# A decoder layer on one core: the gated sum's second half is turned by VectorE and DMAs instead of TensorE, and what follows goes token tile by token tile

## The chip, the core and the metric

The kernel runs on one core of a Trainium2 chip. Weights and activations start in HBM; TensorE multiplies into PSUM, VectorE and ScalarE work on SBUF and PSUM, GpSimd does a little of the attention's preparation, and SP issues nearly all DMAs. The metric is the device time of one execution in microseconds, the median of several runs.

## The reference

One layer on x with 256 tokens and 1024 channels, in float32:

```
h = RMSNorm(x)
x_rnn, g_rnn, q, k, v, g_A, g_B = split(h @ W_in)         # 1024 columns each
A = GeLU(g_rnn) * RG-LRU(causal_conv4(x_rnn))
B = causal attention, 8 heads of 128, q and k normalised  # 256 tokens: one block
y = sigmoid(g_A) * (A @ P_A) + sigmoid(g_B) * (B @ P_B)   # the gated sum
x = x + y @ W_out
h = RMSNorm(x)
x = x + (GeLU(causal_conv3(h @ W_up)) * (h @ W_gate)) @ W_down   # 2816 wide
```

## The kernel before

**Products.** Float32 precision comes from three products. Each number is split into a high part hi (rounded to the short format fp32r that TensorE multiplies) and the rest lo, and a product is hi·hi + hi·lo + lo·hi (`mm3`). A weight chunk is 128x2048 numbers (1 MB): SP loads it as `raw`, ScalarE casts it to `hi`, VectorE subtracts to get `lo`. There are three buffers for raw, four for hi, three for lo. Activations are split in the same way; their parts have names that end in h and l (xgh and xgl, mh and ml, h2h and h2l).

**The start.** `g`, the weights of the first norm (4 KB), is loaded by ScalarE's queue; xT, the transposed input, and the first chunks of the k weights come in small pieces (`raws`) by SP's queue. The first activation, `xgh`, is xT times g, rounded; `xgl` is the rest. While these arrive, TensorE runs 9 warm-up products (`warm`). An explicit load of ScalarE's table for the exponential is one of the first operations recorded.

**Units.** `UNITS` (line 33) lists TensorE's work up to the output projection, one unit per chunk. rx, rg and ri belong to the recurrent branch; q, k, v and the heads' attention to the other; ga and gb are the gates, pr and pa the two branches' projections, wo the output projection. pr, pa and wo have four units each: two halves of the output columns, times two halves of the contraction. A unit has four quarters of 12 products of 128x512. `AFTER` (line 35) says which other pieces of work follow which quarter.

**The gated sum.** pr's columns are gated into `sga`, pa's into `sgb`, and `pa_evac` adds them, both token tiles (t = 0, 1; 128 tokens each) of one half of the columns at a time. wo needs the sum channel by channel on the partitions, so it is turned. The first half goes by `m_turn`: VectorE transposes 32x32 blocks (`md`), four DMAs write them to HBM (`mm`), one reads them back in order. The second half goes by `m_t`, TensorE: 2 times 4 transposes of 128x128 into PSUM (`mT`), each set followed by a cast (mh) and a subtraction (ml) from there. These transposes stand among the products of wo0.

**Behind it.** wo0 and wo1 give the first 512 output columns, wo2 and wo3 the others; VectorE adds them to `xs`. The second norm's input is turned too, the first half of token tile 0 by blocks and DMAs (`hd`, `hm`), that of tile 1 by four TensorE transposes (`h2T`, item n10), from which VectorE makes `h2q`, ScalarE `h2h` and VectorE `h2l`. They are needed by up00, the first unit of the feed-forward part, whose units are up (W_up), gt and the seven-product scheme qA, qB, qC (W_gate), and dn or acc (W_down).

**What sets the order.** Nothing is issued as the code is read. Class `Later` records every operation, TensorE's in one list and all others in another, and `issue` (line 238, in the changed kernel 257) walks through `ORDER`: "+n" stands for the next n TensorE operations, every other number is a recorded operation. So all instructions have the line of `issue`, each engine runs its own in the order of this table, and the pools choose buffers by it. Loads that ScalarE's tables need, where none was asked for, are put in ahead of an activation by the compiler.

Of the kernel before, what the change touches and what calls it, by code (L numbers as in the profile page):

```python
# [14 lines left out]
P = 128  # L15
# [18 lines left out]
         "gb1 gb2 gb3 pr0 pr1 pr2 pa0 pa1 pr3 pa2 pa3 wo0 wo1 wo2 wo3")  # L34
# [60 lines left out]
    "pa2.3": "ms",  # L95
    "pa3.2": "s38",
# [10 lines left out]
    "wo0.1": "m2",  # L107
    "wo0.2": "m3",
    "wo1.0": "s40",
    "wo2.0": "s41",  # L110
    "wo2.1": "n10",
# [3 lines left out]
0 4 1 3 26 28 30 32 2 29 31 +2 5 33-34 +1 7 37-38 6 35-36 +2 8 39-40 +1 10 43-44 9 41-42 +3 47-48 11 45-46 12 49-50 13  # L115
51-52 +5 15 55-56 +5 14 53-54 +13 16 59-60 57-58 18 63 17 65-66 64 61-62 19 67-68 +5 23 74-77 +3 20 224-226 69 24 27
227 25 228-235 71 105-106 236-242 +58 93 72 108 21-22 78 109 79-91 +1 96 +5 99 +37 73 142-143 92 102 95 97 94 117-118
120 119 121-122 243 123-126 244 127-133 +9 110 +3 111-112 101 103-104 187-188 107 190 +9 141 +5 116 115 113-114 98 100
144-156 +10 186 +3 191 157-159 245-247 160 248-254 70 255-262 +20 168 +1 170 169 171-172 175 174 173 135 134 136
204-205 +24 207-208 +10 176-177 182-183 199 184-185 195-197 178-180 200 198 201-202 181 162 161 163 +11 212 +3 213 189  # L120
210-211 137 203 192 139 138 206 +16 222-223 +22 220-221 193-194 267 263 271 264 268 140 166 275-276 +7 282 284 +3 285
269 272 265 270 283 277-278 273-274 219 266 +18 302 +6 304 303 294 299 209 297 295 165 167 164 327 298 279 316 300 +25
281 296 286 280 317-318 +20 301 442 305-306 309 +3 307 334-335 310 330-331 308 214 366 454 367-368 370 369 371-378 315
288 311 314 312-313 215 329 379-382 +6 443 332 339 +6 364 319 321 +6 323 362 324 +6 340 +6 217 338 218 328 +19 342 325
343 444 320 326 322 448 333 452-453 455 216 341 +20 336 357 +3 598 337 358 363 599 612 615 +12 356 +15 360-361 445 +9
359 +12 348-349 346-347 351 461 350 352-353 462 365 344-345 463-468 291 289 355 290 354 398-399 613 469-470 446 434
287 397 410 +26 614 435 +8 437 +2 433 +11 383-384 471-475 +3 393 386 394 385 +3 395-396 387 438 556 617 +11 400-401
389 388 402-403 390-392 494 496-497 495 404 498 292 436 +11 411 447 440 412-416 449 616 421-422 417-420 +11 423
405-406 426 522-524 503 526 525 476-477 424-425 427 +26 441 459 428-430 432 431 407-408 439 +1 456 +2 506 509 508 533
507 510 460 450-451 500 458 409 536-537 539 538 521 +1 293 457 +17 478-480 489 481-482 499 504-505 +4 825 824 540 +18  # L130
490 484 483 485 487 486 551-552 555 488 544 554 553 +13 511-515 534 492 517 502 501 649 535 531-532 516 +3 663 527 +3
529 518 493 +15 491 +8 545 528 542 520 519 530 546-547 648 583 585 587 584 586 548 557 +23 558 543 +9 564 +3 565 +5
569-573 559 549-550 650 567-568 +11 566 600 541 +11 588 575 651 589-590 574 579 576 578 577 580 601 560 602 604 562
# [108 lines left out]
def trunk_layer(ctx: ExitStack, tc: tile.TileContext, xT, x, vec, win_fm, win_tm, wri, wpr, wpa,  # L242
# [1099 lines left out]
```

## Time and profile before

| | |
|---|---|
| time, median of 3 runs | 420.74 us (420.3 to 420.89) |
| profiled execution, first to last instruction | 418.6 us |
| TensorE busy | 414.0 us, 1892 matmuls |
| VectorE busy | 360.9 us, 449 instructions |
| ScalarE busy | 307.5 us, 399 instructions |
| GpSimd busy | 61.0 us |
| DMA traffic | 106.89 MB, mean 255 GB/s |
| table loads on ScalarE | 14, 1283 ns each |

The profile has no end-to-end time of its own for the profiled execution beside its span of 418.6 us; the runs' median is 2.14 us above that. In the rows, "x48" is the number of instructions in a group or in a row of equal ones, and "[2.16 <-DMA xT<-in_xT]" says how long the engine was idle before and what ended it. A row of the chain of waits has its start and its length in us. PE is TensorE, DVE VectorE, ACT ScalarE, POOL GpSimd; SPq and ACTq are the queues that issue DMAs.

### The profile page before, as it was taken

How to read it: one execution, taken by the hardware profiler on the slowest of the kernel's cores; microseconds unless marked ns; L12 is line 12 of the kernel's file. 1: busy time of each engine (PE TensorE's matmuls, PEld its weight loads, DVE VectorE, ACT ScalarE, POOL GpSimd, SP SyncE). 2: the span in 40 equal slices, each digit the busy share in tenths (PEclk: the TensorE clock that was granted, in tenths of full speed). 3: DMA queues.
4: the chain of work that ended last, by engine and by line, in shares of the span. 5: the costliest groups of instructions: out<-in, count | busy, mean ns of one | idle time of the engine just before them, and what ended most of it. 6: DMA issues, size and time to landing. Idle time of an engine off the chain costs nothing.

```text
span 418.6 us, 5425 instructions
## 1 busy us (share of the span) xinstructions
PE 414.0 (99%) x1892; PEld 344.4 (82%) x1892; DVE 360.9 (86%) x449; ACT 307.5 (73%) x399; POOL 61.0 (15%) x109
## 2 busy tenths in 40 slices
PE   8999999999999999999999999999999999999996
PEld 7888888888888888888888888888888888888885
DVE  4877699999999999879896789899999989988863
ACT  4787478799989998796144475699897779866630
POOL 0084780009382002000000000000000000000000
PEclk9999999999999999999999999999999999999999
DMA  7998688979696988797698669575799748649803
GB/s 230 416 397 280 194 258 266 321 241 365 220 317 236 279 277 289 221 357 256 205 353 281 233 200 315 173 219 171 258 328 317 279 152 267 205 148 267 318 2 102
DMA packets 46108, 106.89 MB, mean 255 GB/s; under 512 B 8448, under 2 KB 22656, under 8 KB 43648
## 3 DMA queue, kind: packets, MB, share of 16 engines
q1 hardware_dynamic: 45360, 106.01, 76.1%
q10 hardware_dynamic: 720, 0.53, 0.4%
q8 instruction: 15, 0.25, 0.2%
q14 instruction: 13, 0.11, 0.1%
HBM read 92.63 MB, written 13.89 MB: 254 GB/s over the span
## 4 chain that ended last, share of the span: by engine, by line
PE 98%; DMA 1%; ACT 0%; DVE 0%; SPq 0%; issue 0%; ACTq 0%
PE acc L238 14%; PE up L238 13%; PE k L238 5%; PE gb L238 5%; PE qA L238 5%; PE pr L238 5%; PE wo L238 5%; PE ga L238 5%; PE v L238 5%; PE q L238 5%; PE pa L238 5%; PE rg L238 5%; PE rx L238 5%; PE qC L238 3%; PE gt L238 3%; PE last L238 3%
## 5 line engine op out<-in xcount | busy, mean ns | idle before, releaser
L238 DVE TENSOR_TENSOR lo<-raw,hi 128x2048 fp32r<-128x2048 f32 (+1 forms) x64 | 141.4, 2215 | 9.2 <-ACT hi L238 8.3
L238 ACT CAST hi<-raw 128x2048 fp32r<-128x2048 f32 (+1 forms) x64 | 118.2, 1856 | 29.2 <-DMA raw<-in_wout 16.7
L238 PE MATMUL up<-hi,h2l 128*128 128x512 f32 x80 | 31.1, 389 | 0.0
L238 PE MATMUL up<-hi,h2h 128*128 128x512 f32 x80 | 31.1, 389 | 0.0
L238 PE MATMUL up<-lo,h2h 128*128 128x512 f32 x80 | 31.1, 389 | 0.0
L238 PE MATMUL acc<-hi,fah 128*128 128x512 f32 x78 | 30.4, 390 | 0.0
L238 PE MATMUL acc<-hi,fal 128*128 128x512 f32 x78 | 30.4, 389 | 0.0
L238 PE MATMUL acc<-lo,fah 128*128 128x512 f32 x78 | 30.4, 389 | 0.0
L238 POOL TENSOR_TENSOR rsq<-rsq 128x8 f32<-128x8 f32 x32 | 21.0, 655 | 46.7 <-DVE rsq L238 44.5
L238 ACT ACT_TABLE_LOAD x14 | 18.0, 1283 | 1.4 <-PEq L1332 1.2
L238 PEld LDWEIGHTS up<-hi,h2h 128*128 128x128 f32 x80 | 15.0, 188 | 3.2
L238 PEld LDWEIGHTS up<-hi,h2l 128*128 128x128 f32 x80 | 15.0, 188 | 3.1
L238 PEld LDWEIGHTS up<-lo,h2h 128*128 128x128 f32 x80 | 15.0, 188 | 3.1
L238 PEld LDWEIGHTS acc<-hi,fah 128*128 128x128 f32 x78 | 14.6, 188 | 3.1
L238 PEld LDWEIGHTS acc<-lo,fah 128*128 128x128 f32 x78 | 14.6, 188 | 3.1
L238 PEld LDWEIGHTS acc<-hi,fal 128*128 128x128 f32 x78 | 14.7, 188 | 3.1
L238 DVE TENSOR_TENSOR loq<-wq,hiq 128x1024 fp32r<-128x1024 f32 x12 | 14.5, 1215 | 1.3 <-ACT hiq L238 1.3
L238 ACT ACTIVATE fu<-fupd,pv 128x256 f32<-128x256 f32 x32 | 15.2, 502 | 0.5 <-DVE fc L238 0.3
L238 ACT CAST hiq<-wq 128x1024 fp32r<-128x1024 f32 x12 | 12.3, 1049 | 4.1 <-PE acc L238 2.2
L238 DVE TENSOR_TENSOR wq<-wq,wq 128x1024 f32<-128x1024 f32 x12 | 14.6, 1216 | 0.2
L238 DVE TENSOR_TENSOR lot<-wq,hit 128x1024 fp32r<-128x1024 f32 x12 | 14.4, 1218 | 0.0
L238 ACT CAST hit<-wq 128x1024 fp32r<-128x1024 f32 x12 | 12.2, 1045 | 1.0 <-PE acc L238 1.0
(303 smaller groups left out, 1175.3 us busy)
## 6 DMA issues: line engine op xcount, KB each, us to landing
raw<-in_win_fm SPq DMA_DIRECT2D x16, 1024.0 KB, 7.0
raw<-in_wdown SPq DMA_DIRECT2D x11, 1024.0 KB, 6.1
raw<-in_wup SPq DMA_DIRECT2D x10, 1024.0 KB, 5.9
raw<-in_win_tm SPq DMA_DIRECT2D x8, 1024.0 KB, 6.7
wq<-in_wgate SPq DMA_DIRECT2D x16, 512.0 KB, 6.2
raw<-in_wpr SPq DMA_DIRECT2D x4, 1024.0 KB, 7.6
raw<-in_wpa SPq DMA_DIRECT2D x4, 1024.0 KB, 7.8
raw<-in_wout SPq DMA_DIRECT2D x8, 512.0 KB, 5.4
```

What stands on the lines that cost most here:

```text
L238: getattr(engine, name)(*map(real, a), **{n: real(v) for n, v in k.items()})
```

## The change

It has five parts.

1. `m_t` is gone. For each token tile t there is `m_tile_turn(t)`, which is one VectorE transpose of 128x512 in blocks of 32x32, four DMAs to HBM and one back (by `turn_tile`, which the second norm uses already), and `m_tile_split(t)`, a cast and a subtraction of 128x512 from SBUF. TensorE loses eight transposes.
2. pa's second half and the output projection go token tile by token tile: pa2.0 pa3.0 pa2.1 pa3.1, then wo0 (both tiles) wo2.0 wo1.0 wo2.1 wo1.1 wo3.0 wo3.1; a unit with ".t" has 12 products. Tile 0's turn follows pa3.0, tile 1's pa3.1. `pa_evac` and `norm2` take single tiles.
3. up00 does token tile 1 first.
4. h2T is moved from wo2.1 to wo3.0, that is from 36 products ahead of up00 to 18.
5. `ORDER` is written anew from end to end, so all engines' orders change in many places.

The table moves one operation of ScalarE's start. Operation 4, the explicit table load, stood second ("0 4 1 3"); now it stands behind operations 687 and 690 ("687 690 +2 4 +1 689"). In the rows that follow, a number behind a name tells tiles apart, and DMAHW0, DMAHW1 and so on are the counters of eight DMA lanes, which transfers take in turn. ScalarE's first rows before:

```order
L238 DMA g_77<-in_vec 128x8
L238 ACT_TABLE_LOAD
L238 ACTIVATE xgh_95<-xT_93,g_77 128x256 [waits DMAHW2_49,DMAHW0_49]
L238 CAST his_89<-raws_82 128x512 [waits DMAHW3_49]
L238 CAST his_89<-raws_82 128x512 [waits DMAHW4_49]
```

and now:

```order
L257 DMA g_79<-in_vec 128x8
L257 ACT_TABLE_LOAD [waits DMAHW1_49]
L257 ACTIVATE xgh_96<-xT_85,g_79 128x256 [waits DMAHW0_49]
L257 CAST his_91<-raws_87 128x512 [waits DMAHW3_49]
L257 ACTIVATE xgh_96<-xT_85,g_79 128x256 [waits DMAHW4_49]
```

The load that now stands ahead of xgh is one that the compiler put there, and it carries a wait for lane 1, which is g's transfer; xgh is left with the wait for lane 0, xT's. SP now issues xT ahead of the first raws.

VectorE's rows from the end of the first pa half to the product of pa3 (lo_2081 in the change and lo_2059 before are pa3's chunk, the lo_2076 of the change is wo0's; wt, loq and wq belong to W_gate's product), before:

```order
L238 STREAM_TRANSPOSE md<-sgb_1640 128x8x4x32 [waits DVE_49]
L238 TENSOR_TENSOR wt_2054<-wq_2012,wq_1467 128x1024 [waits DMAHW5_49]
L238 TENSOR_TENSOR loq_2056<-wq_1961,hiq_1963 128x1024
L238 TENSOR_TENSOR wq_1961<-wq_1465,wq_1959 128x1024 [waits DVE_49]
L238 TENSOR_TENSOR lo_2059<-raw_2008,hi_2010 128x2048 [waits DMAHW4_49,Activation_49]
L238 TENSOR_TENSOR sga_1398<-pr_1924,sga_1398 128x512 [waits PE_49]
L238 TENSOR_TENSOR sga_1398<-pr_1928,sga_1398 128x512 [waits PE_49]
L238 TENSOR_TENSOR lo_2115<-raw_2016,hi_2113 128x2048 [waits DMAHW7_49,DMAHW0_49,Activation_49]
L238 TENSOR_TENSOR lo_2120<-raw_2014,hi_2118 128x2048 [waits DMAHW5_49,DMAHW6_49,PE_49,Activation_49]
```

and now:

```order
L257 STREAM_TRANSPOSE md<-sgb_1616 128x8x4x32 [waits DVE_49]
L257 TENSOR_TENSOR lo_2076<-raw_1994,hi_2044 128x2048 [waits DMAHW5_49,DMAHW4_49,Activation_49]
L257 TENSOR_TENSOR lo_2081<-raw_2021,hi_2073 128x2048 [waits DMAHW7_49,PE_49,Activation_49]
L257 TENSOR_TENSOR sga_1455<-pr_1906,sga_1455 128x512 [waits PE_49]
L257 TENSOR_TENSOR sgb_1852<-pa_2064,sgb_1852 128x512 [waits PE_49]
L257 TENSOR_TENSOR sga_1455<-pr_1902,sga_1455 128x512
L257 TENSOR_TENSOR sgb_1852<-sgb_1852,sga_1455 128x512 [waits DVE_49]
L257 STREAM_TRANSPOSE md_2134<-sgb_1852 128x4x4x32 [waits DVE_49]
```

pa3's lo stood behind three operations of W_gate's product and stands now behind wo0's lo; the eviction, addition and turn of the second half's tile 0 follow it.

VectorE's rows between wo's evictions and up00 (h2q, h2l: the turned input of the second norm; lo_2297 in the change and lo_2280 before are up00's chunk), before:

```order
L238 TENSOR_TENSOR h2q<-h2T_2273,pv 128x4x128 [waits PE_49]
L238 TENSOR_TENSOR lo_2280<-raw_2209,hi_2254 128x2048 [waits DMAHW3_49,Activation_49]
L238 TENSOR_TENSOR h2l_2299<-h2q,h2h_2297 128x4x128 [waits PE_49,Activation_49]
L238 SCALAR_TENSOR_TENSOR h2l_2299<-hd_2228,pv,h2h_2297 128x128 [waits DMAHW4_49,Activation_49]
L238 SCALAR_TENSOR_TENSOR h2l_2299<-hd_2228,pv,h2h_2297 128x128 [waits Activation_49]
L238 SCALAR_TENSOR_TENSOR h2l_2299<-hd_2228,pv,h2h_2297 128x128
L238 TENSOR_TENSOR xs<-wo_2259,xs 128x512 [waits PE_49]
```

and now:

```order
L257 TENSOR_TENSOR xs<-wo_2161,xs 128x512 [waits PE_49]
L257 TENSOR_TENSOR lo_2297<-raw_2252,hi_2261 128x2048 [waits DMAHW7_49,Activation_49]
L257 TENSOR_TENSOR xs<-wo_2197,xs 128x512 [waits PE_49]
L257 TENSOR_TENSOR h2q<-h2T_2290,pv 128x4x128
L257 TENSOR_TENSOR h2l_2315<-h2q,h2h_2311 128x4x128 [waits Activation_49]
L257 TENSOR_TENSOR xs<-wo_2240,xs 128x512 [waits PE_49]
L257 STREAM_TRANSPOSE hd<-xs 128x4x4x32 [waits DVE_49]
```

h2q now stands behind a lo and behind the eviction of wo3.0 (xs<-wo_2197); before, it stood ahead of both.

The diff, without the greater part of `ORDER`:

```diff
-         "gb1 gb2 gb3 pr0 pr1 pr2 pa0 pa1 pr3 pa2 pa3 wo0 wo1 wo2 wo3")
+         "gb1 gb2 gb3 pr0 pr1 pr2 pa0 pa1 pr3 pa2.0 pa3.0 pa2.1 pa3.1 wo0 wo2.0 wo1.0 wo2.1 wo1.1 wo3.0 wo3.1")
...
-    "pa2.3": "ms",
-    "pa3.2": "s38",
+    "pa20.3": "ms",
+    "pa30.3": "mt0",
+    "pa31.2": "s38",
+    "pa31.3": "mt1",
...
-    "wo0.1": "m2",
-    "wo0.2": "m3",
-    "wo1.0": "s40",
-    "wo2.0": "s41",
-    "wo2.1": "n10",
+    "wo0.3": "s40",
+    "wo20.3": "ms0",
+    "wo10.0": "s41",
+    "wo21.3": "ms1",
+    "wo30.1": "n10",
...
-0 4 1 3 26 28 30 32 2 29 31 +2 5 33-34 +1 7 37-38 6 35-36 +2 8 39-40 +1 10 43-44 9 41-42 +3 47-48 11 45-46 12 49-50 13
...
++1 0 +3 2-3 5-6 30 +3 29 33 7 20 31 +1 32 9 35 +2 37 +1 47 8 41 12 +1 10 +2 11 224 +1 39 +4 43 14 34 +1 36 225 38 +1 49
...
++1 837 +7 656 +3 669 682 +3 683 +6 684 +4 707 777 685 +3 686 +11 25 +4 680 +1 708 +1 678 681 679 +3 687 690 +2 4 +1
...
-    def pa_evac(g, ps):
-        for t in range(2):
+    def pa_evac(g, ps, ts=range(2)):
+        for t in ts:
             m = tok(sgb, g, t)
             nc.vector.tensor_mul(m, ps[t], m)
             nc.vector.tensor_add(m, m, tok(sga, g, t))
...
-    def m_stat(a, k, t):
-        return head_q(a, k, t) if k < 4 else a[k][:, t * P:(t + 1) * P]
-
-    def m_t(c):
-
-        ps = fm_ps(f"mT{c}")
-        for k2 in range(2):
-            cs = slice((2 * (c % 2) + k2) * P, (2 * (c % 2) + k2 + 1) * P)
-            for t in range(2):
-                nc.tensor.transpose(ps[:, k2, t * P:(t + 1) * P], tok(sgb, c // 2, t)[:, cs], ident)
-        split2(mh.pair(c), ml.pair(c), ps)
+    turned_m1, mid_m1 = half("md1"), dram.tile([P, 1024], F32, tag="turn", name="mm1")
+
+    def m_tile_turn(t):
+        turn_tile("mm1", turned_m1, tok(sgb, 1, t), mid_m1, t)
+
+    def m_tile_split(t):
+        v = lambda a: a.half(1).rearrange("p (u i b) -> p u i b", u=8, i=4)[:, 4 * t:4 * t + 4]
+        split2(v(mh), v(ml), by_tile(turned_m1)[:, 4 * t:4 * t + 4])
...
-    def norm2(hf, ps):
-        for t in range(2):
-            nc.vector.tensor_add(xs[:, t, halves[hf]], ps[t], xs[:, t, halves[hf]])
+    def norm2(t, ps):
+        nc.vector.tensor_add(xs[:, t, halves[1]], ps, xs[:, t, halves[1]])
...
+        if (kind, p, kh) == ("up", 0, 0):
+            for q in range(4):
+                for k4 in (2 * (q % 2), 2 * (q % 2) + 1):
+                    tm_mm(open_ps[kind, p], c, k4, k4, h2h, h2l, True, ts=(1 - q // 2,))
+                yield
+            return
```

More of the change, by code (lines that the diff above doesn't have):

```diff
@@ L153 @@
[L153 to L156 removed]
+1 0 +3 2-3 5-6 30 +3 29 33 7 20 31 +1 32 9 35 +2 37 +1 47 8 41 12 +1 10 +2 11 224 +1 39 +4 43 14 34 +1 36 225 38 +1 49
@@ L157 @@
+805 884 843 +7 820-821 +1 887 +2 852 860 888 +2 859 +1 822 +4 912 +2 890 1045 +1 873 +1 826 +5 853 +2 855 +2 914 +1
[5 rows of a table added]
+982 +2 951 +3 949 +2 958 +8 1017 +3 1005 +1 952 +2 954-955 +2 985 +3 960 +2 1062 1050 908 933 +1 1056-1057 +2 961 +2
+984 +3 1075 1051 1048-1049 +4 1014 +7 1073 1063 +2 965 +2 1064 1058 983 +1 1041 +1 986 +2 964 +4 1065 +3 1074 +1 1066
[10 rows of a table added]
 """
@@ L303, in trunk_layer @@
               "pr": lambda c: two(wpr, 0, c), "pa": lambda c: two(wpa, 0, c), "wo": lambda c: by_columns(wout, c)}
-    units = [(u[:-1], int(u[-1])) for u in UNITS.split()]
-    chunk = {u: add(source[u[0]](u[1])) for u in units}
+    units = [(u[:2].rstrip("0123"), int(u.split(".")[0][-1]), *map(int, u.split(".")[1:])) for u in UNITS.split()]
+    chunk = {}
+    for u in units:
+        if u[:2] not in chunk:
+            chunk[u[:2]] = add(source[u[0]](u[1]))
     NP = NF // 2
@@ L882, in run_unit @@
             g, kh = c // 2, c % 2
-            if not kh:
+            if not kh and ts in ((), (0,)):
                 open_ps[kind, g] = [bank(f"{kind}{g}{t}") if kind in ("pa", "rx") else
@@ L887, in run_unit @@
             args = (*{"pr": (yah, yal), "pa": (ybh, ybl), "wo": (mh, ml)}.get(kind, (xgh, xgl)),
-                    kind not in ("q", "v", "wo"), *((m_stat,) if kind == "wo" else ()))
-            if (kind, c) == ("wo", 1):
-                for q in range(4):
-                    for k4 in (2 * (q % 2), 2 * (q % 2) + 1):
-                        tm_mm(ps, i, 4 * kh + k4, k4, *args, ts=(q // 2,))
-                    if q % 2:
-                        norm2_tile(q // 2, ps[q // 2])
-                    yield
-                return
-            for k4 in range(4):
-                tm_mm(ps, i, 4 * kh + k4, k4, *args)
-                if kh and k4 == 3:
+                    kind not in ("q", "v", "wo"), *((head_q,) if kind == "wo" else ()))
+            for k4 in range(4):
+                tm_mm(ps, i, 4 * kh + k4, k4, *args, **({"ts": ts} if ts else {}))
+                if kh and k4 == 3 and ts:
+                    if kind == "pa":
+                        pa_evac(g, ps, ts)
+                    elif g:
+                        norm2(ts[0], ps[ts[0]])
+                    else:
+                        norm2_tile(ts[0], ps[ts[0]])
+                elif kh and k4 == 3:
                     evac[kind](g, ps) if kind in evac else qk_evac(kind, g, ps)
@@ L919, in trunk_layer @@
             item[f"{n}{h}"] = lambda fn=fn, h=h: fn(h)
-    for n in (2, 3):
-        item[f"m{n}"] = lambda n=n: m_t(n)
+    for t in range(2):
+        item[f"mt{t}"] = lambda t=t: m_tile_turn(t)
+        item[f"ms{t}"] = lambda t=t: m_tile_split(t)
     item["mt"], item["ms"] = m_turn, m_split
@@ L1005, in trunk_layer @@
     item["ht"], item["hs"] = h2_turn, h2_split
-    for kind, c in units:
+    for kind, c, *ts in units:
         if (kind, c) not in (("k", 1), ("k", 2), ("k", 3)):
-            run(f"{kind}{c}", run_unit(kind, c))
+            run("".join(map(str, (kind, c, *ts))), run_unit(kind, c, *ts))
     def norm2_stats():
```

65 lines of the change are left out of this document (22 added, 43 removed), and 34 rows, old and new, of the table ORDER.

## The prediction

> **What bounds the kernel now.** I read the page's busy times first, then the list of TensorE's waits, then the chain of waits; their rows stand below in this order.
>
> ```profile
> PE 414.0 (99%) x1892; PEld 344.4 (82%) x1892; DVE 360.9 (86%) x449; ACT 307.5 (73%) x399; POOL 61.0 (15%) x109
> ...
> PE warm L238 <- DVE ones L238: 1.0, 1, 1.0
> PE k L238 <- ACT xgh L238: 0.4, 1, 0.4
> ...
> 5.16 22.51 PE k L238 x96
> ...
> 217.30 2.73 PE wo L238 x12
> 220.03 0.44 PE mT L238 x4
> 220.46 1.40 PE wo L238 x6
> 221.86 0.44 PE mT L238 x4
> 222.30 9.56 PE wo L238 x42
> 231.86 0.44 PE h2T L238 x4
> 232.29 8.21 PE wo L238 x36
> 240.51 16.32 PE up L238 x72
> ```
>
> TensorE is busy 414.0 of 418.6 us. It waits twice, both times before 5.16 us; from then on one product follows the other. So the time is the moment of the first k product, plus the work of TensorE, plus a short tail. Whatever leaves TensorE's queue is won whole; whatever starts k later is lost whole; anything else counts only where it makes TensorE wait.
>
> **What the change takes from TensorE.** It drops the eight mT transposes, which stand between wo products. From 217.30 to 231.86 pass 14.56 us, with 12 + 6 + 42 = 60 wo products in them. One product takes 10.88/48 = 0.2267 us where nothing disturbs it:
>
> ```profile
> 206.42 10.88 PE pa L238 x48
> ```
>
> 60 of them are 13.60 us, so the transposes and the changes to and fro cost 14.56 - 13.60 = **0.96 us**. No other TensorE work is added or removed: token tile by token tile, pa2, pa3 and wo1 to wo3 have the same products in another order, and the four h2T transposes are only moved. The gain is 0.96 us and, since TensorE never waits now, cannot be more in this place.
>
> **What the change does to the start.** The rewritten table moves one ScalarE operation that has nothing to do with attention: the explicit load of the exponential's table stood second, ahead of everything, and now stands far back, in the pa products. Some table must be there for the first activation, xgh, so a load is put just ahead of it, and that load takes over one of xgh's two waits: the one for g (the norm's weights). The timeline of the start before, and the row of g from the list of transfers (size, us from issue to landing):
>
> ```profile
> 0.71 0.41 ACTq L238 DMA_DIRECT2D g<-in_vec  x1
> 1.03 3.68 PE L238 MATMUL warm<-ones 128*128 128x128 f32 x18 [1.03 <-DVE ones L238]
> 1.15 1.28 ACT L238 ACT_TABLE_LOAD   x1 [1.15 <-PEq L1332]
> 4.60 0.51 ACT L238 ACTIVATE xgh<-xT,g 128x256 fp32r<-128x256 f32 x1 [2.16 <-DMA xT<-in_xT]
> 4.66 0.69 DVE L238 TENSOR_TENSOR los<-raws,his 128x512 fp32r<-128x512 f32 x1
> 5.16 0.73 PE L238 MATMUL k<-his,xgh 128*128 128x512 f32 x2 [0.45 <-ACT xgh L238]
> 5.27 0.48 DVE L238 SCALAR_TENSOR_TENSOR xgl<-xT,g,xgh 128x256 fp32r<-128x256 f32 x1
> 6.90 0.73 PE L238 MATMUL k<-his,xgh 128*128 128x512 f32 x2
> ...
> g<-in_vec ACTq DMA_DIRECT2D x1, 4.0 KB, 3.6
> ```
>
> Before, the 1.28 us of the load lay under the transfers, and xgh waited 2.16 us longer. Now the load waits itself. g is issued at 0.71 and lands 3.6 later, at 4.31; it cannot land later than 4.60, when xgh read it. So the load runs from 4.31 to 5.59. How soon an activation follows a load is shown by two later rows of ScalarE's timeline:
>
> ```profile
> 121.86 1.28 ACT L238 ACT_TABLE_LOAD   x1
> 123.16 1.06 ACT L238 ACTIVATE gr<-gr 128x1024 f32<-128x1024 f32 x1
> ```
>
> 0.02 us. Then xgh takes 0.51, to 6.12, and the first product starts 0.05 later (5.11 to 5.16 before), at **6.17 us: 1.01 later**. VectorE follows: xgl began 0.16 after xgh's end, so 6.28 to 6.76; los, which before was finished ahead of xgl, is now queued behind it and ends at 7.45. Products five and six need los: the fifth starts at 7.50, the seventh at 7.95 instead of 6.90, 1.05 later. TensorE waited for nothing behind that in k, and everything ahead of the later products has a microsecond more now, so the rest keeps its pace.
>
> I take **+1.00 us**. Bounds: +1.3 if g lands only at 4.60; below, nothing at all, if g were there by 3.3 us and the load ended as xT lands. The row for g says 4.31, so the value lies near the upper end.
>
> The Trainium skill, "ScalarE: Activation LUTs", section "What ACT_TABLE_LOAD costs", puts a switch at about 1.28 us of load and 1.38 us of drain. The load agrees with the 1.28 here; a drain ahead of the next activation doesn't show in the 0.02 us above. By the page the start would come another 1.38 later, and the sum would be 422.2.
>
> **What the change adds on the other engines.** Two VectorE transposes of 128x512 come (0.71 each, by the row of hd<-xs below); the two casts and two subtractions of this half of m keep their number and size. SP gets ten DMAs, eight writes and two reads like those of hm and hd below. The windows of before, by stage:
>
> ```profile
> core 0: us, PE busy (x) PEld busy (x) DVE busy (x) ACT busy (x) POOL busy (x), PEclk, DMA share, GB/s
> 200.00:232.00 32.00, 32.00 (x148) 26.49 (x147) 27.62 (x27) 12.31 (x10) 0.00 (x0) 1.00 0.81 268
> 232.00:262.00 30.00, 30.00 (x135) 24.84 (x134) 25.07 (x37) 18.47 (x29) 0.00 (x0) 1.00 0.76 264
> ...
> 303.00:345.00 42.00, 42.00 (x186) 34.71 (x186) 39.68 (x33) 33.82 (x40) 0.00 (x0) 1.00 0.79 273
> ```
>
> VectorE is idle for 9.3 of the 62 us from 200 to 262, so 1.42 us more fit. What covers them is slack between a result and its product, and the change uses that up at four places. I give times as without the later start, which moves all of it alike. Durations come from the groups of instructions, the timelines and the list of transfers:
>
> ```profile
> L238 DVE TENSOR_TENSOR lo<-raw,hi 128x2048 fp32r<-128x2048 f32 x10 | 22.8, 2286 | 0.2 <-ACT hi L238 0.2
> L238 DVE STREAM_TRANSPOSE hd<-xs 128x512 f32<-128x512 f32 x3 | 2.1, 711 | 0.1
> ...
> 200.34 1.37 DVE L238 TENSOR_TENSOR sgb<-pa,sgb 128x512 f32<-128x512 f32 x2 [2.31 <-PE pa L238]
> ...
> 202.94 1.25 DVE L238 STREAM_TRANSPOSE md<-sgb 128x1024 f32<-128x1024 f32 x1
> ...
> 227.92 1.78 SPq L238 DMA_DIRECT2D hm<-hd  x4
> ...
> hm<-hd SPq DMA_DIRECT2D x4, 64.0 KB, 1.8
> hd<-hm SPq DMA_DIRECT2D x1, 256.0 KB, 3.1
> ...
> 233.11 0.68 DVE L238 TENSOR_TENSOR h2q<-h2T,pv 128x512 f32<-128x512 f32 x1
> 233.83 0.62 ACT L238 CAST h2h<-h2q 128x512 fp32r<-128x512 f32 x1 [2.59 <-DVE h2q L238]
> 235.91 0.69 DVE L238 TENSOR_TENSOR h2l<-h2q,h2h 128x512 fp32r<-128x512 f32 x1
> ```
>
> First, pa3's first token tile comes 12 products (2.72 us) earlier, at 206.42 + 2.72 = 209.14, and its lo is needed 0.23 later. VectorE does the first half's eviction and addition from 200.34 to 202.94, its turn to 204.19, then two lo of 2.29 that overlap a little, the second of them this one: done near 208.7. Slack 0.6.
>
> Second, the turn of tile 0: pa's second half for it ends at 211.86; eviction, an sga product, addition and transpose are four operations of about 0.7; the four writes take 1.78 to issue and the last of them 1.8 to land, the read 3.1, the cast 0.62, the subtraction 0.69: about 222.5, needed at 225.9. Slack 3.
>
> Third, tile 1: it starts at 217.30, its way back waits in SP's queue behind a wup chunk, and its subtraction stands on VectorE behind the eviction of wo1's first tile (wo1.0 ends at 228.18): done about 230.3, needed at 231.35. Slack 1.
>
> Fourth, h2T is moved from 36 products ahead of up00 to 18. up00 would start at 240.51 - 0.96 = 239.55. Its h2q stands on VectorE behind a lo (2.29, from about 234.4 to 236.7) and behind the eviction of wo3.0, which ends 12 products earlier, at 236.83: eviction to 237.6, h2q 0.68, h2h on ScalarE 0.62, h2l 0.69: h2h near 238.9, h2l near 239.6, needed at 239.55 and 240.0. Slack 0.4 to 0.7, where before h2l was done at 236.6 for a product at about 241, over 4 us ahead.
>
> I cost all four at nothing. Cover gone, each is a stall of its own length; behind 303 us VectorE is busy 39.68 of 42, so a lo that is late once stays late, but its number of operations there is unchanged.
>
> **Sum.** 418.6 - 0.96 + 1.00 = 418.64 us of span. The median, 420.74, lies 2.14 above the profiled span; with it, **420.8 us**: no change.
>
> **The rivals.** (A) *The start costs nothing*: g is there early enough, and the load ends when xT lands. Then 420.74 - 0.96 = 419.8, faster. For it: SP's first transfers come in another order, and with less traffic beside it g may land sooner; against it: the 3.6 us of its row, on its own queue, and nothing that moved on that queue. 17 of 100.
>
> (B) *up00 waits for h2l*, slower. Place: the fourth one above. If the lo ahead of h2q begins one operation late (its hi is cast from a chunk whose load is queued behind the turn's way back on SP), the chain moves by up to a lo, 2.29, less the slack of 0.5: up to 1.8 us, and the same mechanism can hit at the first or third place with 1.7 and 1.3. It decides from 0.8 us of stall on. Time 421.6 to 423, middle 422.2. For it: slack under 1 us at three places where nothing was tight before; against: every chain still closes on paper. 27 of 100.
>
> (C) *The clock falls back.* Between the end of the warm products (4.71) and the first k product TensorE idles 1.45 us instead of 0.45. If the clock falls to half for 3.4 us, 7.5 products take 0.45 instead of 0.227: +1.7, 422.5. Every row of before shows PEclk 1.00, and no gap like it. 5 of 100. The Trainium skill, "TensorE: Matmul & The Clock Gate", section "What's actually happening", speaks of about 3.4 us of idling before the clock drops, by which this gap is too short; no run so far shows either.
>
> (D) *A pause behind the load*: xgh waits once more as long as the load took, 1.28 us, at the start, where nothing covers it: 420.8 + 1.3 = 422.1. The 0.02 us at 123.16 speaks against it. 4 of 100. It is the drain of the Trainium skill's page "ScalarE: Activation LUTs", section "What ACT_TABLE_LOAD costs".
>
> **How the numbers follow.** The forecast, TensorE's gain given back at the start and no stall above 0.5, has 47 of 100: 420.8, its own range 420.2 to 421.5. A has 17, B 27, C and D 9. A change of 0.2%, 0.84 us, is about what a measurement here can tell from none: faster means under 419.90, slower over 421.58. A gives faster, 0.17; the forecast gives no change, 0.47, and B, C and D slower, 0.36. The range leaves out the upper part of B and the lower of A: 419.7 to 422.6.
>
> **What would show it.** In the changed profile: no mT rows; the first table load waits for g's transfer and starts near 4.3 instead of 1.15, xgh near 5.6, the first k product near 6.2; from there to up00 about 0.96 less than the 235.35 of before (5.16 to 240.51). TensorE's waits then list k behind xgh with about 1.4 us. If up, pa or wo stands in that list with 0.8 us or more, B is right; if k starts by 5.3, A; if the granted clock of the first 10 us is under 1.00, C; if xgh begins over 1 us behind the load's end, D.

## The result: about one per cent slower

The changed kernel takes 424.74 us (424.72 to 425.01), the kernel before 420.78 us beside it: a ratio of 1.0097, 95% interval 1.0083 to 1.0112. The forecast was 420.8, its range 419.7 to 422.6: too low, and the range doesn't hold the time.

The profiled execution has a span of 422.9 us, 4.3 more than before. Its page, the busy times:

```profile
PE 415.2 (98%) x1884; PEld 343.0 (81%) x1884; DVE 359.4 (85%) x451; ACT 305.2 (72%) x397; POOL 55.8 (13%) x109
```

The eight transposes are gone (1884 products, 1892 before), but the busy time didn't fall by 0.96 us, and the idle time of TensorE grew from 4.6 to 7.7 us. (A product that waits for its weights can count as busy, so the two numbers belong together.) The list of waits of the changed kernel (what waited, for whom, us in total, times, the longest), TensorE's products first, then its weight loads:

```profile
PE k L257 <- ACT his L257: 1.5, 1, 1.5
PE s L257 <- ACT sm L257: 1.1, 2, 0.7
...
PE k L257 <- DVE his L257: 0.6, 1, 0.6
...
PEld k L257 <- ACT his L257: 3.3, 5, 1.9
PEld s L257 <- ACT sm L257: 1.6, 2, 1.0
...
PEld acc L257 <- DVE lo L257: 0.6, 2, 0.4
```

k, the scores `s` and, a little, `acc` (W_down's products) wait; up, pa and wo don't. The chain of waits of the changed kernel (start, length, what), a part of k and then the place of the change:

```profile
4.02 6.70 DMA raws<-in_win_tm
10.73 8.67 DMA raws<-in_win_tm
...
21.78 8.90 PE k L257 x38
...
211.16 10.88 PE pa L257 x48
222.04 17.68 PE wo L257 x78
...
240.16 4.10 PE wo L257 x18
244.26 16.32 PE up L257 x72
```

Before, k's 96 products stood in this chain as one row from 5.16 on; now loads of k's weights stand in it up to 19.40. The time is best followed by the first product of each group, read from the timelines of the two kernels (us):

| first product of | before | after | difference | since the row above |
|---|---|---|---|---|
| k | 5.16 | 5.32 | +0.16 | +0.16 |
| rx | 27.51 | 30.52 | +3.01 | **+2.85** |
| pr (behind the gates and most of attention) | 171.75 | 176.49 | +4.74 | **+1.73** |
| wo | 217.14 | 221.88 | +4.74 | 0 |
| up | 240.34 | 244.10 | +3.76 | **-0.98** |
| acc (W_down) | 314.14 | 317.93 | +3.79 | +0.03 |
| last (the final chunk) | 352.39 | 356.49 | +4.10 | **+0.31** |
| end (the final products) | 413.86 | 417.93 | +4.07 | -0.03 |

Behind that another 0.24 us come (4.31 of span). They aren't the table's: in every profile of the changed computation here, whichever order it has, the span ends 5.00 to 5.02 us behind the start of the first `end` product, in every profile of the computation before 4.76 to 4.78 us. So the change wins what it takes from TensorE, and the rewritten table loses five times that at places that have nothing to do with the change's first four parts: 2.85 us within k, 1.73 at the gates, 0.31 at W_down.

These rows compare one execution with one. The 93 timed executions of the kernel before have spans from 418.5 to 419.6 us, the middle at 419.0; the profiled one, with 418.6, is among the shortest. So a difference against it, here and below, can lie some 0.3 us too high, and the medians, 3.96 us apart, are the better measure of the whole.

**The start.** The changed kernel's timeline (start, length, engine, operation, idle time before it and what ended it):

```profile
3.19 1.28 ACT L257 ACT_TABLE_LOAD   x1 [3.19 <-DMA xT<-in_xT]
4.48 0.51 ACT L257 ACTIVATE xgh<-xT,g 128x256 fp32r<-128x256 f32 x1
4.75 0.43 DVE L257 CAST his<-raws 128x512 fp32r<-128x512 f32 x1 [3.75 <-DMA raws<-in_win_tm]
...
5.32 0.70 PE L257 MATMUL k<-his,xgh 128*128 128x512 f32 x2 [0.57 <-DVE his L257]
```

The load of the table waits for xT, not for g. The prediction and the section on the change took lane 1 for g's; the lanes are counted in the order of issue, so g has lane 0 and xT, now SP's first transfer, lane 1. xT lands at 3.1, and the load begins at 3.19; before, as SP's second transfer, xT ended xgh's wait at 4.60. So the load lies behind xT, and yet xgh begins 0.12 us earlier than before. A wait for g would have cost nothing either. Its row in the changed kernel:

```profile
g<-in_vec ACTq DMA_DIRECT2D x1, 4.0 KB, 2.6
```

Issued at 0.73, g is there at 3.33, a microsecond earlier than before (3.6 from its issue). The load had begun by then, so it can't have waited for g; had it done so, it would have ended at about 4.6. k waits for `his` instead, because the first piece of its weights was put behind xT: 0.16 us.

**Within k.** Three rows of the same timeline:

```profile
8.52 0.91 ACT L257 ACTIVATE xgh<-xT,g 128x256 fp32r<-128x256 f32 x2 [0.34 <-DMA xT<-in_xT]
...
10.74 0.62 ACT L257 CAST his<-raws 128x512 fp32r<-128x512 f32 x1 [1.31 <-DMA raws<-in_win_tm]
...
11.41 0.74 PE L257 MATMUL k<-his,xgh 128*128 128x512 f32 x2 [1.51 <-ACT his L257]
```

ScalarE is idle 1.31 us until a piece of weights lands, casts it, and TensorE has waited 1.51 for that. Five weight loads of TensorE wait in this way, 3.3 us together. The pieces take longer to come: the list of transfers before (KB each, median us from issue to landing) and after, and the first 15 us in windows (length, PE, PEld, DVE, ACT and POOL busy, clock, DMA share, GB/s):

```profile
raws<-in_win_tm SPq DMA_DIRECT2D x8, 256.0 KB, 5.1
raws<-in_win_tm SPq DMA_DIRECT2D x4, 512.0 KB, 7.5
...
0.00:15.00 15.00, 13.52 (x59) 11.08 (x60) 7.87 (x15) 8.68 (x14) 0.90 (x6) 1.00 0.85 287
```

and of the changed kernel:

```profile
raws<-in_win_tm SPq DMA_DIRECT2D x8, 256.0 KB, 6.7
raws<-in_win_tm SPq DMA_DIRECT2D x4, 512.0 KB, 9.0
...
0.00:15.00 15.00, 11.88 (x52) 9.52 (x53) 6.75 (x13) 7.27 (x14) 2.14 (x9) 1.00 0.85 253
```

At the same busy share of the DMA engines, 253 GB/s come instead of 287: 0.5 MB less in 15 us, about two pieces of k's weights.

**At the gates.** TensorE and ScalarE of the changed kernel around the scores of head 6 (161 to 162) and head 7 (166 to 167):

```profile
161.06 0.28 PE L257 MATMUL s<-kT,qTh 128*128 128x256 f32 x1
161.73 0.27 ACT L257 COPY sm<-s 128x128 f32<-128x128 f32 x1
162.05 0.33 PE L257 MATMUL s<-kT,qTl 128*128 128x128 f32 x1 [0.71 <-ACT sm L257]
...
166.53 0.27 ACT L257 COPY sm<-s 128x128 f32<-128x128 f32 x1 [0.46 <-PE s L257]
166.85 0.39 PE L257 MATMUL s<-kT,qTh 128*128 128x256 f32 x1 [0.35 <-ACT sm L257]
```

The scores of a head are five products into one PSUM tile. Before, ScalarE copies from that tile behind all five, for every head. In the new table, the copy of the second 128 columns stands behind the first product of head 6 and behind the third of head 7. The next product into the tile waits until the copy is through (161.73 + 0.27 = 162.00), and the copy itself stands on ScalarE behind two operations of 0.7 us. The Trainium skill, "PSUM — Partial Sum Buffer", section "PSUM bank collisions raise a hardware error", says that the compiler makes any two instructions of different engines on the same bank and quadrant wait for each other, reads too; the 0.71 and 0.35 us here agree.

### The profile page after: what moved, and what is told of

Its sections match the earlier page's. It is cut to its first block, busy times and chain, and to the rows that moved or that the text cites. A ratio compares the mean times of both kernels' runs of the same rounds, so it can differ in the third digit from the quotient of the medians.

```text
span 422.9 us, 5440 instructions
## 1 busy us (share of the span) xinstructions
PE 415.2 (98%) x1884; PEld 343.0 (81%) x1884; DVE 359.4 (85%) x451; ACT 305.2 (72%) x397; POOL 55.8 (13%) x109
## 4 chain that ended last, share of the span: by engine, by line
PE 86%; ACT 5%; DMA 4%; DVE 3%; issue 2%; SPq 1%; ACTq 0%; DVEq 0%
PE acc L257 14%; PE up L257 13%; PE qA L257 5%; PE pr L257 5%; PE q L257 5%; PE wo L257 5%; PE pa L257 5%; PE rg L257 5%; PE rx L257 5%; DMA raws<-in_win_tm 4%; PE ga L257 3%; PE qC L257 3%; PE gb L257 3%; PE gt L257 3%; PE last L257 3%; PE v L257 3%
## 5 line engine op out<-in xcount | busy, mean ns | idle before, releaser
L257 DVE TENSOR_TENSOR los<-raws,his 128x512 fp32r<-128x512 f32 (+1 forms) x12 | 10.3, 868 | 7.9 <-ACT his L257 7.9
L257 ACT CAST hit<-wq 128x1024 fp32r<-128x1024 f32 x12 | 12.5, 1052 | 6.1 <-PE up L257 4.1
```

What stands on the lines that cost most here:

```text
L257: getattr(engine, name)(*map(real, a), **{n: real(v) for n, v in k.items()})
```

## The experiments

Three groups: which part of the table costs k its 2.85 us; whether the copies cost the scores; whether the change's 0.98 us can be had alone. In all of them only `ORDER` is changed. A name that begins with b_ is the kernel before with a part of the change, one that begins with a_ is the changed kernel with a part undone. Of each kernel one execution was profiled; where its time is far from the median, the text says so.

The loads of k's phase by SP, by their numbers in the table (2, 6, 9, 14 and 17 are parts of xT, 20 is pv, the small vectors; the others are pieces of k's weights):

```
before: 3 2 5 7 6 8 10 9 11 12 13 15 14 16 18 17 19 20
after:  2 3 5 6 7 20 9 8 12 10 11 14 13 15 17 16 19 18
```

### One load early: b_pv

Before SP loads pv behind k's weights, in the change as its sixth transfer. The kernel before with that alone:

```diff
-+1 7 37-38 6 35-36
++1 7 20 37-38 6 35-36
...
-+3 20 224-226
++3 224-226
```

> The kernel before, with one operation moved: the load of pv (85 KB of small vectors) goes from behind the k weights to the fifth place of SP's queue, between the first pieces, where the changed kernel has it. Theory P (pv alone fills a place among the eight transfers that may be under way and pushes the weights back): k ends about 2 to 3 us later, 422.8 to 423.8 us. Theory O (the order of the weights' own pieces does it, pv little): within 0.6 us of 420.8.

Measured: 420.60 us (420.20 to 420.97), ratio 0.9997 (0.9987 to 1.0006). No cost.

### All loads: b_sp

The kernel before, with SP's loads of k's phase at the head of the table in the changed order (the second list above); the conversions keep the order of before.

> The kernel before, with SP's loads of xT, the k weights and pv in the changed kernel's order; everything on the other engines, the early table load too, stays. If SP's order is the whole cause of the 3.0 us that k lost, this takes 423.4 to 423.9 us. If the order on ScalarE and VectorE, or the later table load, is the cause, it stays at 420.8 to 421.2.

Measured: 423.24 us (422.19 to 424.10), ratio 1.0059 (1.0042 to 1.0077): +2.5 us. The profiled execution, the fastest of the four, has rx at 29.27 instead of 27.51.

### The early order undone: a_k

The changed kernel with the order of before, on every engine, up to the last k product (9 warm-up and 96 k products); behind it the changed order.

> The changed kernel, with the order of the kernel before on all engines up to the last k product, and its own from there. If the loss at the start is a shift and nothing more, 424.74 - 3.0 = 421.7 us. If the later start hid other waits, which transfers set and not TensorE, part of it comes back as new waits: 422.3 to 424.

Measured: 422.17 us (422.15 to 422.37), ratio 1.0037 (1.0023 to 1.0051): against the kernel before beside it +1.45, so 2.51 of the change's 3.96 us are gone. rx starts at 27.97. Kernels with the early order of before have it between 27.39 (h840) and 28.21 (best1140), so nothing of the loss within k is left; the copies at the scores are in the list of waits as they were.

### Which loads: b_sp_nopv, b_sp_tail, b_xt, b_w

Each is the kernel before with one list of loads at the head of the table:

```
b_sp_nopv: 2 3 5 6 7 9 8 12 10 11 14 13 15 17 16 19 18 20
b_sp_tail: 3 2 5 7 6 8 9 12 10 11 14 13 15 17 16 19 18 20
b_xt:      3 2 5 7 6 8 9 10 11 12 14 13 15 17 16 18 19 20
b_w:       3 2 5 7 6 8 12 10 9 11 13 15 14 16 19 17 18 20
```

The first is the changed order without the early pv, the second keeps the first six loads of before, the third moves only parts of xT forward, the fourth only changes the order of weight pieces.

> The kernel before, with SP's loads of xT and the k weights in the changed kernel's order, but pv behind them all. If the order of the pieces (xT ahead of the weights that are needed at once) does the harm, as with pv among them, 423.2 us. If it takes pv and the order together, 420.8 to 421.5.

> The kernel before, with its own order of the first seven loads and the changed kernel's order of the loads behind them (the second piece of the second chunk ahead of the first, xT's last parts ahead of weights), pv last. If the harm is done by the first loads, 420.8; if by those behind, 422 to 423.

> The kernel before, with only xT's last three parts (256 KB each) one or two places earlier in SP's queue, ahead of weights; the weights keep their order among themselves. If k is bound by the arrival of the weights, and what is loaded ahead of need pushes them back, 421.4 to 422.4 us (each part is 0.65 us at 400 GB/s). If the weights' own order does the harm, 420.8.

> The kernel before, with only the weights' order in SP's queue changed as in the changed kernel (the second chunk's third piece ahead of its first, the last two pieces exchanged); xT's parts keep their places. If it is this that makes k wait, 421.4 to 422.4 us; if it is xT's parts, 420.8.

| | median, us | ratio (95%) |
|---|---|---|
| b_sp_nopv | 423.11 | 1.0062 (1.0047 to 1.0077) |
| b_sp_tail | 422.98 | 1.0049 (1.0032 to 1.0066) |
| b_xt | 420.94 | 1.0004 (0.9995 to 1.0013) |
| b_w | 421.53 | 1.0019 (1.0010 to 1.0028) |

The first six loads and pv are not it: the tail has nearly all of the 2.5 us. Within the tail, the parts of xT alone cost nothing, the weight pieces alone 0.7, both together 2.2. So it is no single load; the two orders cost most of it only together. (b_xt also shows that writing the loads at the head of the table costs nothing by itself.) These kernels have the loads' order changed against the conversions' order, though: in b_sp the weight loads of TensorE wait most for xgl (1.4 us) and his (1.0), in the change for his (3.3) and los (1.2). That b_sp loses as much as a_k wins back is therefore not proof that it loses it in the same way.

### Loads undone in the change: a_8, a_sp

a_8 moves one load, a piece of weights, ahead of pv, so that SP issues it earlier:

```diff
-29 33 7 20 31 +1 32 9 35 +2 37 +1 47 8 41
+29 33 7 8 20 31 +1 32 9 35 +2 37 +1 47 41
```

> The changed kernel, with one load of its start moved: the fourth quarter of the first k chunks (256 KB) goes ahead of pv and of xT's second part in SP's queue, two places earlier, as in the kernel before. If its late arrival (10.72 us; TensorE waits for it to 11.41) is what k loses most, the first wait of 1.5 us goes: 423.0 to 423.5 us. If every later piece is late for its own reason, 424.2 to 424.8.

Measured: 424.29 us (422.90 to 425.00), ratio 1.0074 (1.0060 to 1.0089). Against before +3.54, so 0.42 us come back, less than the runs scatter. The profiled execution is the slowest of the four (425.00), and its rx starts at 30.61, no earlier than in the change. ScalarE's timeline of it:

```profile
9.76 0.91 ACT L257 ACTIVATE xgh<-xT,g 128x256 fp32r<-128x256 f32 x2 [1.89 <-DMA xT<-in_xT]
10.57 2.17 ACT L257 CAST his<-raws 128x512 fp32r<-128x512 f32 x4
```

The piece is there now, but xT is later (its third part is ready at 9.76; the change's xgh could use it at 8.52), and the piece's cast stands, with three others, behind the xgh that waits 1.89 us for it.

a_sp has all of SP's loads in the order of before (the first list) and leaves the conversions of the change as they are.

> The changed kernel, with SP's loads of the k weights, xT and pv in the order of the kernel before; ScalarE and VectorE keep the changed order. If the order of the loads is the whole loss at the start, 424.74 - 2.6 = 422.1 us. If the order in which ScalarE and VectorE take the pieces costs too, 422.8 to 424.

Measured: 430.54 us (429.79 to 431.26), ratio 1.0234 (1.0221 to 1.0247): 5.8 us worse than the change. ScalarE's timeline of a_sp:

```profile
19.74 0.21 ACT L257 ACTIVATE decw<-decw 128x8 f32<-128x8 f32 x1 [5.12 <-POOL decw L257]
```

pv comes late again, and a small operation of the recurrent branch that hangs on it (decw), which the new table puts early on ScalarE, holds three casts for 5.12 us. Two more things are in the 5.8 us: the table load waits for an xT that is SP's second transfer again (next section; the first product starts at 6.50, 1.18 later than in the change), and the clock falls during the wait for the casts (last section). Here the order of before for the loads alone, without that of the conversions, is worse than either table.

### The table load alone: b_tab

The kernel before, with the explicit table load (operation 4) moved back as in the change:

```diff
-0 4 1 3 26 28 30 32
+0 1 3 26 28 30 32
...
-687
+687 4
```

> The kernel before, with one operation moved: the explicit table load goes from ScalarE's second place to where the changed kernel has it, so that the load ahead of xgh waits for g. By the prediction's step (g lands at 4.3, the load follows, k starts 1.0 later) 421.7 us. By the trace of the change (the load began at 3.19 and was over before xT could be used) the k weights set the start and it stays at 420.7.

Measured: 421.48 us (421.32 to 423.06), ratio 1.0030 (1.0018 to 1.0042). Its timeline, ScalarE and TensorE:

```profile
4.66 1.28 ACT L241 ACT_TABLE_LOAD   x1 [4.66 <-DMA xT<-in_xT]
...
6.51 0.73 PE L241 MATMUL k<-his,xgh 128*128 128x512 f32 x2 [1.27 <-ACT xgh L241]
```

So the prediction's step is a real mechanism, by another transfer: the load that the compiler puts in waits for xT, where xT comes second in SP's queue it waits until 4.66, and the first product is at 6.51, 1.35 late. 1.06 of that are still there at rx, 0.74 in the median. In the change xT comes first, 1.4 us earlier, and hides the load again.

### The copies at the scores: a_s, and both: a_ks

The changed kernel, with the remaining products of heads 6 and 7 issued ahead of the copy:

```diff
-+1 527 569 +2 570 +2 616 567
++1 527 +4 569 570 616 567
...
-+1 568 588 575 +1 579 +2 589
++1 568 +2 588 575 579 +1 589
```

> The changed kernel, with the five products of the attention scores of heads 6 and 7 issued together, ahead of ScalarE's copy from the same PSUM tile; in the changed order that copy stands between them. If that copy is what TensorE waits for at 161 and 166 us, both waits go: 424.74 - 1.6 = 423.1 us. If the softmax chain behind it sets the time anyway, 424.2 to 424.8.

Measured: 423.44 us (421.92 to 423.66), ratio 1.0057 (1.0039 to 1.0076): against before +2.72, so 1.24 us come back, and no score waits any more. From rx to pr the delay grows by 0.30 us (rx +1.60, pr +1.90) instead of 1.73. (The profiled execution is the fastest of the four, 421.92, and had lost less within k; the growth from rx to pr doesn't depend on that.)

> The changed kernel with both mends at once: the order of the kernel before up to the last k product, and the score products of heads 6 and 7 issued together. The two gains measured one by one are 2.57 and 1.30 us. If they are separate losses, they add: 420.7 to 420.9 us. If one wait covers the other's, 421.5 or more.

a_ks makes both edits, a_k's and a_s's: 420.68 us (420.40 to 421.15), ratio 0.9998 (0.9989 to 1.0007). Alone they win back 2.51 and 1.24 us, together 4.07, all of the change's 3.96. The two losses add up within the scatter. What remains is the kernel that the prediction spoke of, and it is as fast as before: the 0.95 us won from wo to up (up stands at -0.32 against before, wo at +0.63) pay for 0.3 at rx, 0.3 at the gates, 0.33 at W_down, where the lead is gone (acc -0.23, last +0.10), and the 0.24 behind the last product. At least the 0.3 at rx are rather those of one execution than of the order. The first products of a_ks:

```profile
1.03 4.21 PE L256 MATMUL warm<-ones 128*128 128x128 f32 x18 [1.03 <-DVE ones L256]
5.22 1.18 PE L256 MATMUL k<-his,xgh 128*128 128x512 f32 x2
```

The 18 warm-up products take 4.21 us here and 3.68 before, the first two of k 1.18 and 0.73. In both kernels the warm-up products start 0.21 us apart at first. In the kernel before they start 0.11 apart from 4.0 us on, so the full clock comes there; in a_ks it comes only within k. (The windows show a clock of 1.00 from the start in both, which the products contradict.)

### The gain alone: pre_mid_before, h840, h840_plain, h840_us, best1140, best1368

These join parts of the two tables at a number of TensorE operations: up to there the order of before, behind it the order of the change (which holds the change's own place). pre_mid_before: before up to 956, the change up to the end of up00, then before again. h840: before up to 840, then the change, with two moves in the feed-forward part, a cast (hi, 1003) earlier and a transpose (928) behind that chunk's lo (1004). h840_plain: the same without these moves. h840_us: h840, and `us` (1052, an update on VectorE) behind the lo (1072) that follows it:

```diff
 h840 against h840_plain
-896 948 ... 1003 +1 902 1006 904 928 +1 ... 1004
+1003 896 948 ... +1 902 1006 904 +1 ... 1004 928
 h840_us against h840
-+5 1052 +4 947 +4 1072
++9 947 +4 1072 1052
```

best1140 and best1368: before up to 840, the change up to 1140 (1368), then before.

> The changed kernel's computation (turn by VectorE and DMAs, token tile by token tile, later h2T, up00 by tiles), with the order of the kernel before up to the projections pr and pa, the changed kernel's order from pa2 to the end of up00, and the order of the kernel before from there. If the change itself brings TensorE's 0.96 us and the table around it lost the rest, 419.8 us. If the turn or the later h2T makes waits of its own, 420.5 or more.

> The changed kernel's computation, with the order of the kernel before up to the middle of pr2 (840 products; at this place both orders have done nearly the same work on VectorE and ScalarE), then the changed order, in which the lo that the first down product waited for stands one place earlier and its hi too. Nothing is left of the three places that lost time, so the change's own gain should show: 420.74 - 0.96 = 419.8 us. If the turn of the second half or the later h2T cost something that the other losses hid, 420.4 or more.

> As h840, but with the changed order of the feed-forward part left as it is. The changed kernel lost 0.3 us there, at two lo. If TensorE's lead of 0.96 us makes no new wait, 0.6 of it is left at the last product and the time is 420.3 us; if VectorE bounds this part, so that any lead beyond the changed kernel's own is given back there, 420.7 to 421.3 as in h840.

> As h840, with one operation of VectorE moved: the addition into us (0.74 us) goes behind the lo for which the third down chunk's products waited 1.14 us. If that lo is the last thing in the way, 0.7 us of the wait goes: 420.6 us. If VectorE as a whole is late there, the wait turns up at the next lo, 421.0 to 421.3.

> The changed kernel's computation, in the order of the kernel before up to 840 products, the changed order to the middle of up1, and the order of the kernel before for the rest of the feed-forward part. If the change's own 0.96 us is kept by an order of VectorE that has no late lo behind it, 419.8 us; if the seam makes TensorE wait, 420.5 or more.

> The same, with the second seam later, in the middle of gt21, just ahead of the place where the changed order's lo came late. 419.8 us if the gain is kept; 420.5 or more if the seam makes TensorE wait.

| | median, us | ratio (95%) | up against before | acc | last |
|---|---|---|---|---|---|
| pre_mid_before | 427.67 | 1.0167 (1.0152 to 1.0182) | +5.82 | +6.67 | +6.67 |
| h840 | 421.31 | 1.0013 (1.0004 to 1.0022) | -0.96 | -0.88 | +0.14 |
| h840_plain | 420.61 | 0.9997 (0.9987 to 1.0006) | -0.54 | -0.40 | -0.04 |
| h840_us | 420.67 | 0.9998 (0.9989 to 1.0007) | -0.43 | -0.34 | +0.02 |
| best1140 | 423.91 | 1.0084 (1.0063 to 1.0105) | -0.20 | +5.67 | +5.71 |
| best1368 | 431.14 | 1.0245 (1.0232 to 1.0258) | -0.36 | +7.65 | +10.65 |

The columns behind the ratio are differences of first products in the profiled execution, in us; best1140's is the slowest of its six (426.47). Three of the kernels measure their seam, not the change. In pre_mid_before the first seam lies at the start of pa's second half, and the list of waits has, at the first product of wo,

```profile
PE wo L245 <- ACT mh L245: 3.2, 1, 3.2
```

(the read of the turned sum stood on SP behind loads of W_out that waited for their buffers); best1140 waits at up for a lo (1.3 us) and h2l (0.6), best1368 at acc for fah (6.4), and behind these waits the clock is halved for a while (last section). They show only that the two tables don't fit together at any place.

h840 answers the question. Its lead at up is the change's whole gain, 0.96, and it is gone by `last`. Of h840, TensorE's weight load that waits, and VectorE ahead of it:

```profile
344.37 0.19 PEld L250 LDWEIGHTS acc<-lo,fah 128*128 128x128 f32 x1 [1.14 <-DVE lo L250]
...
341.37 0.74 DVE L250 SCALAR_TENSOR_TENSOR us<-qB,rs,us 128x512 f32<-128x512 f32 x1
342.04 2.28 DVE L250 TENSOR_TENSOR lo<-raw,hi 128x2048 fp32r<-128x2048 f32 x1
```

A weight chunk of W_down waits for its lo, which is the last of a row of VectorE operations without a pause. h840_us takes `us` out from ahead of that lo, h840_plain leaves the feed-forward part as the change has it; both lose 0.36 from acc to last, h840 1.02. The runs allow two readings. Either `last` can't come sooner than VectorE lets it: it starts between 352.35 and 352.53 in these three and in a_ks, whatever the lead at acc was (0.23 to 0.88). Or the order of the change costs some 0.3 us there at any time, since the change (0.31), a_k (0.30) and a_s (0.30) lose as much without any lead, and h840 lost the rest by `us`. VectorE in the windows of before, 310 to 355 us:

```profile
310.00:355.00 45.00, 45.00 (x199) 37.10 (x199) 41.77 (x37) 36.25 (x45) 0.00 (x0) 1.00 0.77 259
```

and of h840_plain:

```profile
310.00:355.00 45.00, 45.00 (x198) 36.65 (x197) 43.07 (x33) 37.26 (x46) 0.00 (x0) 1.00 0.71 234
```

VectorE is busy 43.07 of 45 us, 1.30 more than before, and a lo that is late has nowhere to catch up. Three tables without the losses at k and at the scores, a_ks, h840_plain and h840_us, win 0.95 us from wo to up, and all three are at the time of before; none is faster. Counted from rx on, h840_plain and h840_us are still 0.43 and 0.33 us ahead of before at `end`; the 0.24 behind the last product take most of that, and what is left is less than the runs can tell. Whether another order of VectorE's work at W_down would keep the 0.96 us wasn't tried.

## Why the prediction was wrong, by its own steps

**What bounds the kernel**: right, also for the changed one. Every difference in the table of first products is a wait of TensorE or a removed transpose.

**The transposes, -0.96 us**: right, -0.98 in the change from the first wo to the first up product, between -0.94 and -0.98 in a_k, a_s, a_ks and h840.

**The start, +1.00**: the size was wrong, 0.16, for two reasons. I gave the load's wait to the wrong transfer: xT's, not g's, and the change moves xT to the head of SP's queue. And I took g's 3.6 us from the kernel before, where in the change it lands after 2.6; with the wait for g the load would have hidden too, by the lower bound that the prediction itself gives (g there by 3.3). Rival A's outcome (the load hides) is what happened there, through the other order of SP's first transfers that A names, and b_tab shows that the price is real, 1.35 us at the first product, where xT isn't moved. The sentence that failed beside it is the next one, "the rest keeps its pace". I had seen that SP's first transfers come in another order (it stands in rival A) and followed that order for the first activation only. The order of the loads and of the conversions over the next 20 us costs 2.85 us by the profile, 2.51 by a_k.

**Four places at nothing**: right, all of them. pa, wo and up are not in the list of waits. Rival B, the likeliest loser, had the right kind of event (a product that waits for a lo behind VectorE's other work) at places where it didn't come; it came at W_down, 0.31 us, which the prediction touched only with "a lo that is late once stays late".

**What was missing**: the change's fifth part, the table written anew "from end to end", got no term in the sum. The waits at the scores, 1.73 us by the profile and 1.24 by a_s, come from two copies in the middle of five products, visible in the table at two heads of eight. The case "slower" had 36 of 100, but its mechanisms were others: of the 4.0 us nearly all come from places that I hadn't looked at. The range ended at 422.6 because every bound in it belonged to the four places and the load.

**C and D**: the clock stayed at 1.00 through the wait of 1.51 us within k, and xgh began 0.01 us behind the load (3.19 + 1.28 = 4.47, 4.48). (That every row of before shows a clock of 1.00, as C says, doesn't hold for the products of the first 4.0 us, which start at half the later rate.) There is no drain at the start either, against the Trainium skill's "ScalarE: Activation LUTs", section "What ACT_TABLE_LOAD costs"; the load's 1.28 us agree with it.

**What stays open**: which pair of load and conversion sets the loss within k (it takes several at once); which of the two readings holds for the 0.3 us at W_down; why the DMA engines moved 253 instead of 287 GB/s at a busy share of 0.85; and what in the changed computation makes its span end 0.24 us later behind the last products.

## What to carry to other kernels

When a change rewrites the order of everything, the edit that it is about is the smallest part: put the two orders side by side engine by engine, and look for loads that stand in another order than the conversions that read them, and for reads of a PSUM tile that have moved in between the products that write it. A wait that the compiler hangs on another instruction is read by its counter's transfer, counted in the order of issue, not by what seems natural. A gain of a microsecond on the bounding engine has to be followed to the end of the span: here 0.36 us were lost again at W_down, beside a VectorE busy 43 of 45 us, and 0.24 behind the last product. And a difference of a few tenths between two profiles is first compared with the spread of the same kernel's executions, here 1.1 us.

## What the hardware showed that was not expected

**A short wait can halve the clock.** In a_sp TensorE waited 3.35 us for a cast. Its products, and the windows behind them (the number ahead of DMA share is the granted clock):

```profile
16.54 0.61 PE L257 MATMUL k<-los,xgh 128*128 128x512 f32 x2
20.51 1.22 PE L257 MATMUL k<-his,xgh 128*128 128x512 f32 x2 [3.35 <-ACT his L257]
...
19.00:19.50 0.50, 0.00 (x0) 0.00 (x0) 0.00 (x0) 0.00 (x0) 0.34 (x2) 0.92 0.99 410
20.50:26.00 5.50, 5.49 (x13) 4.38 (x14) 4.67 (x7) 5.50 (x8) 4.84 (x11) 0.50 1.03 419
26.00:27.00 1.00, 1.00 (x5) 0.77 (x5) 1.00 (x2) 1.00 (x2) 1.00 (x2) 0.88 1.01 418
```

By the mean of 0.92 in its window, the clock falls to half at about 19.4, 2.3 us into the wait, and it stays there for over 5.5 us of work: 13 products in 5.49 us, 0.42 each instead of 0.227, so that a wait of 3.35 us costs about 2.5 more. The wait of 1.51 us in the change left the clock at 1.00. In best1140 a shorter one was enough:

```profile
259.41 0.50 PE L245 MATMUL up<-hi,h2h 128*128 128x512 f32 x1
261.25 0.50 PE L245 MATMUL up<-lo,h2h 128*128 128x512 f32 x1 [1.33 <-DVE lo L245]
262.38 0.79 PE L245 MATMUL up<-hi,h2l 128*128 128x512 f32 x1 [0.63 <-DVE h2l L245]
...
261.00:262.00 1.00, 0.50 (x1) 0.19 (x1) 1.00 (x2) 0.00 (x0) 0.00 (x0) 0.89 0.93 246
262.00:264.00 2.00, 1.62 (x4) 1.33 (x5) 1.97 (x3) 0.00 (x0) 0.00 (x0) 0.50 0.96 247
268.00:270.00 2.00, 2.00 (x9) 1.55 (x9) 0.99 (x2) 0.08 (x1) 0.00 (x0) 0.85 0.83 328
```

By the 0.89 of its window the clock fell at about 261.8, when the wait of 1.33 us and a product of 0.50 lay behind TensorE and the second wait had only begun. In best1368 it fell 5.1 us into the wait of 6.4 (the window from 320 to 321 us has 0.76). And of best1140's six executions three have a mean clock of 0.999 or 1.000 and take 423.15 to 423.30 us, two have 0.995 and 0.996 and take 424.52 and 424.73, and the profiled one has 0.992 and takes 426.47. So the length of a wait alone doesn't tell whether or when the clock falls, and the same kernel pays for it in some executions only.

The Trainium skill, "TensorE: Matmul & The Clock Gate", section "What's actually happening", lets the clock fall after an idle window of about 3.4 us. Neither case agrees as it stands: TensorE had been idle for 2.3 us in the first and 1.33 us in the second, so by these rows the window needn't be wholly idle.

**The order of loads changes their rate.** The same loads in another order moved 0.5 MB less in the first 15 us at an equal busy share, and the first xT landed 2.4 us after its issue where it stood first in SP's queue, 3.3 where it stood second. g, on a queue of its own, landed after 2.5 to 2.6 us where SP begins with xT, after 3.6 to 3.9 where it begins with a piece of weights.

In the first 20 us the kernels with SP's order of before (before itself, a_k, a_sp, b_tab) move 309 to 318 GB/s, b_xt 317, b_w 307, and those with the order of the change or its tail (the change, a_s, a_8, b_sp, b_sp_nopv, b_sp_tail) 291 to 296. In a_sp, whose products are the latest of all, it is 315: the rate goes with the order of the loads, not with the progress of the products.

At most eight transfers are under way at once in the traces of before and of the change. In the kernel before, the twelfth to the twentieth are each issued within 0.02 us of the landing of the one eight places ahead (landings at 6.21, 7.38 and 10.38 us, issues at 6.22, 7.39 and 10.39). So a load that moves forward can also change when later ones start.
